# A decoder layer on one core: cache pages addressed from registers and read by SyncE, K pages one at a time, V pages in two held sets, feed-forward groups of 6, 8 and 8, last normalisation on VectorE

## The chip, the core and the metric

The kernel runs on one core of one Trainium2 chip. Its engines are TensorE (PE, matmuls, with PEld for loading the stationary operand), VectorE (DVE), ScalarE (ACT), GpSimd (POOL) and SyncE (SP, which here only issues DMAs); each runs its own list of instructions in order, and semaphores join them. The metric is the device time of one execution in microseconds, given as the median of three.

## The reference

One inference step of one layer, in float32, for 512 prompt rows and 8 sample rows (one new token each), width 1024. Every weight matrix is read once.

```python
att = _moba_prompt(aq, ak, av)                       # 8 heads of 64, blocks of 256 keys
h, (C, n, m) = _mlstm_prompt(mq, mk, mv, ig, lf)     # 4 heads of 128, log-sigmoid forget gate
mix = jnp.concatenate([att, mem], axis=-1) @ w_out
x = _layernorm(ALPHA * x + (1.0 + g1[:, None, :]) * mix, ln1_g, ln1_b)
h = x * (1.0 + sc2[:, None, :]) + sh2[:, None, :]
f = (jax.nn.silu(h @ w_gate) * (h @ w_up)) @ w_down  # D_FF = 2816
return _layernorm(ALPHA * x + (1.0 + g2[:, None, :]) * f, ln2_g, ln2_b)
```

The sample rows do the same, but their attention reads a paged cache: `cache_k[page_table]` and `cache_v[page_table]`, 4 pages of 128 keys x 8 heads x 64 for each of 8 rows. That is 32 K pages and 32 V pages of 256 KB, at addresses that are known only when the page table has been read.

## The kernel before

**The main line.** TensorE multiplies float32 numbers as three passes over a high and a low part. Each tile of weights (128 x 1024 numbers) is loaded by SyncE into one of six `raw` buffers (L185), ScalarE casts it to `whi` (L228), another engine subtracts to get `wlo` (L229), and the raw buffer is free again. L229 runs on VectorE, but for tiles 8 to 13 on GpSimd (`PT_`). The main blocks (`wstat_block` L631, `astat_block` and the products of the output and feed-forward stages, whose matmuls stand at L387) use one tile after the other: first the input projections (aq, ak, av, mq, mk, mv, mo), then the output product, then 22 feed-forward tiles with their down products in three groups of tiles (`FF_GROUPS`), then the layer normalisation of the four row tiles. Between the main tiles come side tiles of the adaLN weights (`ps_ada`).

**The lanes.** All else is written as Python generators, called lanes. A main block calls `tick()` after each of its pieces; a tick lets every lane go one `yield` further, prepares one weight tile (two ahead of the one in use) and asks for loads as raw buffers come free. So the order of instructions on each engine is fixed when the program is written, by the ticks. `yield n` waits n ticks; `slot(pool, ...)` waits until a pool has a free buffer (13 halves of 128 x 512 numbers, 22 units of twice that).

**The sample attention.** `sample_scores(b)` handles row b's K pages. It takes four halves, issues four page reads, and some ticks later gives GpSimd four multiplies by the broadcast query in a row (L1202); VectorE then sums them per head. `page` (L1183, its DMA at L1184) is an indirect DMA of GpSimd, with row numbers `idx` worked out beforehand on VectorE. `sample_attention` follows: softmax over the scores, then the products `ps_pv` of the V pages on TensorE (L1289), in eight steps (two groups of rows, four pages each). A step fetches four pages into halves that it takes when there are four free, at most two steps ahead, waits `lag_v` = 4 ticks from its fetch and gives the halves back.

**Its neighbours.** At the same time run the prompt's block attention (its transposed probabilities `ps_pt` on TensorE, copied by VectorE at L827), the mLSTM heads (`ms_unit`: rows `negM` read from DRAM by SyncE, masked by GpSimd at L1013, exponentials on ScalarE, L1027 on VectorE; `mlstm_num` for the numerators), the gates (`log_sigmoids`) and the sample rows' mLSTM states (L1331 to L1334 and L1399 on VectorE).

**The end.** `down_last` makes the last group's down product, tile after tile of rows, half after half of columns. Results are evacuated by VectorE (L1578, L1579: times the gate, plus the residual); `ln2_tile` normalises, dividing the scale and shift (`lg`, `lb`) among ScalarE, GpSimd and VectorE; `ln2_last` does the last tile, and in it one addition (L1854) for the tile before. `affine8` does the sample rows' scale and shift on GpSimd.

## Time and profile before

| what | value |
|---|---|
| median of three runs | 816.4 us (813.91 to 821.64) |
| the profiled execution, its own time | 814.67 us |
| its span, first to last instruction | 813.0 us |
| mean granted TensorE clock | 0.972 |
| busy: TensorE, VectorE, ScalarE, GpSimd | 757.7, 407.1, 277.9, 229.6 us |
| DMA | 123.10 MB, mean 151 GB/s |

In the profile, L12 is line 12 of the kernel before. A row of a timeline has the start in us, the duration in us, the engine, the line and operation with output and inputs by name, how many follow each other, and in brackets the idle time before it with what ended that. A row of groups has the count, the busy time, the mean in ns, and the idle time before. A row of a single line or tile has ns as min/median/max. A row ending in "issue" waited for nothing that the profile shows; "remote" and "another core or an unknown queue" mean that the releaser isn't among the recorded instructions. SPq is SyncE's sequencer. A row of SyncE's waits has the total in us, how often, and the longest.

### The profile page before, as it was taken

To read this page: it belongs to the slowest core of one execution; us is meant where nothing else is said; L and a number is where in the kernel's file an instruction comes from. 1 tells how busy PE (TensorE), PEld (TensorE's weight loads), DVE (VectorE), ACT (ScalarE), POOL (GpSimd) and SP (SyncE) were. 2 spreads that over 40 slices of the span, in tenths; PEclk is the share of its full clock that TensorE was granted. 3 is DMA by queue.
4 is the path that set the end of the run, shared out by engine and by line. 5 is a ranking of instruction groups with operands and counts; after the bars stand their busy time and mean duration, and the time that the engine had idled before them with its cause. 6 is when DMAs were issued, how large, how long until landed. Compare 5 with 4: busy or idle time off the path is not lost.

```text
span 813.0 us, 14321 instructions
## 1 busy us (share of the span) xinstructions
PE 757.7 (93%) x5760; PEld 621.5 (76%) x5760; DVE 407.1 (50%) x851; ACT 277.9 (34%) x555; POOL 229.6 (28%) x244
## 2 busy tenths in 40 slices
PE   5999999698989898899999999999999999999992
PEld 4788667587756575566699998789999877999772
DVE  2551667955534867367855443333333333433585
ACT  2331557434323336346462232122223212222201
POOL 2021579786140326000008700221000022100055
PEclk9999999899999899799999999999999999999997
DMA  8956775566396767646352533233323223321011
GB/s 339 358 206 212 229 251 162 159 212 204 111 290 183 210 218 216 251 148 208 106 164 78 120 116 130 80 103 92 90 80 103 78 78 104 112 96 53 1 40 67
DMA packets 101948, 123.10 MB, mean 151 GB/s; under 512 B 8362, under 2 KB 65838, under 8 KB 101882
## 3 DMA queue, kind: packets, MB, share of 16 engines
q1 hardware_dynamic: 88722, 96.27, 37.1%
q0 software_dynamic: 5184, 16.79, 6.7%
q10 hardware_dynamic: 7976, 9.13, 3.5%
q8 instruction: 45, 0.74, 0.4%
q14 instruction: 21, 0.17, 0.1%
HBM read 114.99 MB, written 7.17 MB: 150 GB/s over the span
## 4 chain that ended last, share of the span: by engine, by line
PE 77%; DVE 12%; DMA 3%; issue 2%; ACT 2%; another core or an unknown queue 1%; POOL 1%; SPq 0%; ACTq 0%; POOLq 0%; DVEq 0%
PE acc L631 35%; PE acc L387 27%; DMA vpage<-in_cache_v_dram,idx 2%; PE ps_ada L401 2%; PE ps_dn L409 1%; PE accl L387 1%; PE ps_sc L789 1%; PE ps_pt L819 1%; DVE x L1579 1%; PE ps_pv L1289 1%; PE ps_ada L455 1%; PE ps_o L842 1%; DVE wlo L229 1%; PE ps_s L401 1%
## 5 line engine op out<-in xcount | busy, mean ns | idle before, releaser
L229 DVE TENSOR_TENSOR wlo<-raw,whi 128x1024 fp32r<-128x1024 f32 x98 | 126.3, 1297 | 115.4 <-ACT whi L228 112.3
L228 ACT CAST whi<-raw 128x1024 fp32r<-128x1024 f32 x104 | 108.3, 1049 | 165.4 <-PE acc L387 80.7
L631 PE MATMUL acc<-h_hi,whi 128*128 128x256 f32 (+1 forms) x640 | 129.8, 284 | 0.0
L631 PE MATMUL acc<-h_hi,wlo 128*128 128x256 f32 (+1 forms) x640 | 128.4, 282 | 0.0
L631 PE MATMUL acc<-h_lo,whi 128*128 128x256 f32 (+1 forms) x640 | 128.2, 282 | 0.0
L631 PEld LDWEIGHTS acc<-h_hi,whi 128*128 128x128 f32 x640 | 99.2, 188 | 2.2 <-issue 2.1
L631 PEld LDWEIGHTS acc<-h_lo,whi 128*128 128x128 f32 x640 | 99.5, 188 | 0.0
L631 PEld LDWEIGHTS acc<-h_hi,wlo 128*128 128x128 f32 x640 | 98.8, 188 | 0.0
L1733 POOL COPY fsT<-vf 128x8 f32<-128x8 f32 x20 | 4.8, 241 | 192.3 <-DVE vf L1728 192.3
L387 PE MATMUL acc<-whi,f_hi 128*128 128x512 f32 x128 | 51.6, 404 | 0.0
L387 PE MATMUL acc<-whi,f_lo 128*128 128x512 f32 x128 | 50.4, 394 | 0.0
L387 PE MATMUL acc<-wlo,f_hi 128*128 128x512 f32 x128 | 50.3, 393 | 0.0
L1202 POOL TENSOR_TENSOR kpage<-kpage,qb 128x512 f32<-128x512 f32 x32 | 40.9, 1306 | 29.6 <-DMA qb<-r_scr 25.8
L1579 POOL TENSOR_TENSOR x<-x,rtmp 128x512 f32<-128x512 f32 x16 | 26.0, 1647 | 77.3 <-DVE rtmp L1578 77.0
L1727 DVE TENSOR_TENSOR vf<-acc,vf 128x256 f32<-128x256 f32 x20 | 8.5, 425 | 74.6 <-PE acc L631 74.6
L387 PE MATMUL acc<-whi,hT_hi 128*128 128x512 f32 x96 | 43.4, 452 | 0.0
L631 PE MATMUL acc<-hT_hi,whi 128*128 128x256 f32 (+1 forms) x160 | 36.8, 310 | 3.5 <-remote 1.8
L1184 POOL DMA_INDIRECT vpage<-in_cache_v_dram,idx x32 | 32.1, 1002 | 27.6 <-DVE own L1243 12.1
L1184 POOL DMA_INDIRECT kpage<-in_cache_k_dram,idx x32 | 33.1, 1035 | 21.5 <-DVE gw L898 13.0
L387 PE MATMUL acc<-wlo,hT_hi 128*128 128x512 f32 x96 | 39.0, 406 | 0.0
L387 PE MATMUL acc<-whi,hT_lo 128*128 128x512 f32 x96 | 38.8, 404 | 0.0
L393 ACT CAST f_hi<-vf 128x512 fp32r<-128x512 f32 (+1 forms) x24 | 14.0, 585 | 68.4 <-DVE vf L1728 62.4
(408 smaller groups left out, 1492.1 us busy)
## 6 DMA issues: line engine op xcount, KB each, us to landing
...
```

Of the source, the lines that this page charges most:

```text
L228: ACOPY(out=t.hi_t, in_=t.raw)
L229: (PT_ if 8 <= t.index < 14 else TT)(out=t.lo_t, in0=t.raw, in1=t.hi_t, op=ALU.subtract)
L387: mm(ps, lhsT=a, rhs=b, start=start and i == 0, stop=stop and i == n - 1)
L393: ACOPY(out=dst_hi, in_=v)
L401: mm(ps[32 * c:32 * c + 32, 0:P], lhsT=lhs[:, k0 + kk, :], rhs=raw3[:, kk, ts(c, P)], start=start and kk == 0, stop=stop and kk == nk - 1, ...
L409: mm(ps[32 * c:32 * c + 32, 0:256], lhsT=lhs[:, k0 + kk, :], rhs=raw3[:, kk, ts(n, 256)], start=start, stop=stop, tile_position=(0, 32 * c))
L455: mm(ps[32 * c:32 * c + 32, 0:w], lhsT=siluT[:, k, :], rhs=rhs, start=k == 0, stop=k == 7, tile_position=(0, 32 * c))
L631: mm(accs[d, hf][:, 0:hi - lo], lhsT=w, rhs=two(xx, k)[:, lo:hi], start=k == 0 and i == 0, stop=k == 7 and i == 2)
L1184: nc.gpsimd.indirect_dma_start(out=dst, out_offset=None, in_=src, in_offset=bass.IndirectOffsetOnAxis(ap=idx[:, 4 * b + j:4 * b + j + 1], ...
L1202: PT_(out=ks[j], in0=ks[j], in1=qb, op=ALU.mult)
L1579: (PT_ if pool_add else TT)(out=dst, in0=dst, in1=tmp, op=ALU.add)
L1727: TT(out=v[:, 0:HALF], in0=a[:, 0:HALF], in1=v[:, 0:HALF], op=ALU.mult)
```

## The change

1. **Pages.** `page` reads the page's number from the table in SBUF into a register of SyncE and issues a plain DMA at that address from SyncE. The page table is loaded as one row, and `idx` with its preparation is gone.
2. **K pages.** `sample_scores` asks for one page a tick (ticks 0 to 3 of its ten), multiplies one a tick on GpSimd (4 to 7) and sums one a tick on VectorE (6 to 9).
3. **V pages.** Two sets of four buffers (one of two units, one of four halves) are taken once. Both are filled as soon as the scores are done; set i is filled again with step i+2 right behind the products of step i. `lag_v` is 5.
4. **Subtractions.** L229 runs on VectorE for all tiles.
5. **Gates and numerators.** `log_sigmoids` uses two activations of ScalarE in place of an operation of VectorE, with one tick less; `mlstm_num` yields after both halves.
6. **Feed-forward.** The groups are 6, 8 and 8 tiles. `down_last` makes the first two row tiles together for each half of the columns, as the weights come in, and then the other two as before; three tiles ahead are prepared only from the last tile on, and splits may then use raw buffers.
7. **Last normalisation.** All four affine steps of a tile are on VectorE; the sample rows are normalised on ScalarE, with the affine on VectorE; `ln2_last` has no addition for the tile before.

On GpSimd, the part with the second half of the K pages. `kpage` is a K page's buffer, `qb` the broadcast query, `wlo` the low part of a weight tile, `gt` the gates. Before:

```order
41 L1184 DMA kpage<-in_cache_k_dram,idx 128x512 x4
42 L229 TENSOR_TENSOR wlo<-raw,whi 128x1024
43 L1202 TENSOR_TENSOR kpage<-kpage,qb 128x512 x4
44 L960 DMA out_dram<-gt_1469 4x1
45 L961 DMA m_scr<-gt_1470 4x512
46 L1184 DMA kpage<-in_cache_k_dram,idx 128x512 x4
47 L229 TENSOR_TENSOR wlo<-raw,whi 128x1024
48 L1202 TENSOR_TENSOR kpage<-kpage,qb 128x512 x4
```

The same place on GpSimd now, up to the masks of the mLSTM heads (`E`):

```order
28 L1200 TENSOR_TENSOR kpage<-kpage,qb 128x512 x20
29 L956 DMA out_dram<-gt_1604 4x1
30 L957 DMA m_scr<-gt_1605 4x512
31 L1200 TENSOR_TENSOR kpage<-kpage,qb 128x512 x12
32 L1009 TENSOR_TENSOR E<-negM,mask_t 128x128 x6
```

Page reads and subtractions are gone from GpSimd's list; the 32 multiplies follow each other with two DMAs between, each behind its own page.

On SyncE, from the gate rows of the first mLSTM head (`negM`) to those of the second. `raw` is a weight buffer, `m_...` are sample states. Before:

```order
75 L1115 DMA negM<-m_scr 128x512
76 L1391 DMA m_2545<-in_state_n_dram 8x512
77 L185 DMA raw<-in_w_in_dram 128x2x512
78 L1393 DMA m_2543<-r_scr 8x512
79 L1394 DMA m_2544<-r_scr 8x512
80 L185 DMA raw<-in_w_ada_dram 128x2x512
81 L185 DMA raw<-in_w_in_dram 128x2x512
82 L185 DMA raw<-in_w_ada_dram 128x2x512
83 L1115 DMA negM<-m_scr 128x512
```

SyncE now, the end of the same stretch; the four page reads are of the first set filled again (`pt_i` is the page table):

```order
241 L185 DMA raw<-in_w_in_dram 128x2x512
242 L1181 TENSOR_LOAD pt_i
243 L1181 ISA x2
244 L1182 ISA
245 L1182 DMA vpage<-in_cache_v_dram 128x512
246 L1181 TENSOR_LOAD pt_i
247 L1181 ISA x2
248 L1182 ISA
249 L1182 DMA vpage<-in_cache_v_dram 128x512
```

Two more pages follow in the same way, and `negM` of the second head stands behind them. A page is five instructions in SyncE's list, and weights and gate rows queue behind it.

The diff, cut:

```diff
@@ -38,7 +38,7 @@
 N_HALVES = 13
-FF_GROUPS = ((0, 8), (8, 16), (16, 22))
+FF_GROUPS = ((0, 6), (6, 14), (14, 22))

@@ -220,13 +220,15 @@
                 src_hi, src_lo = units, units
+            elif state["load"] == len(stream) and len(raws.free) >= 2:
+                src_hi, src_lo = raws, raws
             else:
...
             ACOPY(out=t.hi_t, in_=t.raw)
-            (PT_ if 8 <= t.index < 14 else TT)(out=t.lo_t, in0=t.raw, in1=t.hi_t, op=ALU.subtract)
+            TT(out=t.lo_t, in0=t.raw, in1=t.hi_t, op=ALU.subtract)
             t.hi = t.hi_t.rearrange("p (k c) -> p k c", k=t.k)
@@ -272,9 +274,6 @@
     make_identity(nc, ident)
-    iota_p = cst.tile([P, 1], F32, name="iota_p")
-    nc.gpsimd.iota(iota_p, pattern=[[0, 1]], base=0, channel_multiplier=1,
-                   allow_small_or_imprecise_dtypes=True)
     siluT = cst.tile([P, KD, 32], F32, name="siluT")
@@ -360,8 +359,7 @@
     nc.gpsimd.memset(mhalf, -0.5)
-    pt_i = cst.tile([P, 32], I32, name="pt_i")
-    idx = cst.tile([P, 32], I32, name="idx")
+    pt_i = cst.tile([1, 32], I32, name="pt_i")
     ng = cst.tile([P, 512], F32, name="ng")
@@ -369,7 +367,7 @@
     def later_loads():
-        dma(out=pt_i, in_=row_bc(page_table, 0, 32))
+        dma(out=pt_i, in_=at(page_table, 0, [[0, 1], [1, 32]]))
         dma(out=wg, in_=win[:, :, 3584:3592])
@@ -377,7 +375,6 @@
     def later_consts():
-        TS(out=idx, in0=pt_i, scalar1=128.0, scalar2=iota_p[:, 0:1], op0=ALU.mult, op1=ALU.add)
         nc.gpsimd.tensor_scalar(out=ng, in0=ng, scalar1=0.5, scalar2=None, op0=ALU.mult)
@@ -877,10 +874,9 @@
         for out, z, tmp in jobs:
-            STT(out=tmp, in0=z, scalar=-1.0, in1=z, op0=ALU.mult, op1=ALU.min)
-        yield 1
+            ACT(out=tmp, in_=z, func=AF.Abs)
         for out, z, tmp in jobs:
-            ACT(out=tmp, in_=tmp, func=AF.Exp)
+            ACT(out=tmp, in_=tmp, func=AF.Exp, scale=-1.0)
         for out, z, tmp in jobs:
@@ -1048,8 +1044,7 @@
                        start=jt == 0, stop=jt == t)
-            if half == 0:
-                yield 1
+            yield 1
         num_done[h] = True
@@ -1177,12 +1172,14 @@
     cv = cache_v.rearrange("l n p h d -> (l n p) (h d)")
+    n_phys = cache_k.shape[1]
     mixsT = cst.tile([P, KD, 32], F32, name="mixsT")
...
     def page(dst, src, b, j):
-        nc.gpsimd.indirect_dma_start(out=dst, out_offset=None, in_=src,
-                                     in_offset=bass.IndirectOffsetOnAxis(ap=idx[:, 4 * b + j:4 * b + j + 1], axis=0))
+        i = 4 * b + j
+        n = nc.sync.value_load(pt_i[0:1, i:i + 1], min_val=0, max_val=n_phys - 1)
+        dma(out=dst, in_=src[bass.ds(n * P, P), :])

@@ -1193,21 +1190,22 @@
         qb = yield from slot(halves, "qb")
-        ks = yield from slot(halves, "kpage", n=4)
         dma(out=qb, in_=row_bc(r_scr, b * 512, 512))
-        for j in range(4):
-            page(ks[j], ck, b, j)
-        yield (3, 2, 3, 2)[b // 2]
-        for j in range(4):
-            PT_(out=ks[j], in0=ks[j], in1=qb, op=ALU.mult)
-        halves.put(qb)
-        yield (2, 3, 11, 3)[b // 2]
-        for j in range(4):
-            nc.vector.tensor_reduce(out=SC[:, j, ts(b, 8)], in_=ks[j].rearrange("p (h d) -> p h d", d=64),
-                                    axis=AX, op=ALU.add)
-            halves.put(ks[j])
-            if j % 2:
-                yield 1
+        ks = []
+        for i in range(10):
+            if i < 4:
+                ks.append((yield from slot(halves, "kpage")))
+                page(ks[i], ck, b, i)
+            if 4 <= i < 8:
+                PT_(out=ks[i - 4], in0=ks[i - 4], in1=qb, op=ALU.mult)
+            if i == 7:
+                halves.put(qb)
+            if i >= 6:
+                j = i - 6
+                nc.vector.tensor_reduce(out=SC[:, j, ts(b, 8)], in_=ks[j].rearrange("p (h d) -> p h d", d=64),
+                                        axis=AX, op=ALU.add)
+                halves.put(ks[j])
+            yield 1
         sc_done[0] += 1
@@ -1220,6 +1218,18 @@
             yield 1
+        vu = yield from slot(units, "vpage", [2, 512], n=2)
+        vh = yield from slot(halves, "vpage", n=4)
+        sets = [two(vu, i) for i in range(4)], vh
+        asked = {}
+
+        def fetch(i):
+            for c in range(4):
+                page(sets[i % 2][c], cv, 4 * (i // 4) + c, i % 4)
+            asked[i] = clock[0]
+
+        fetch(0)
+        fetch(1)
         qk = yield from slot(halves, "qk8", n=2)
@@ -1273,22 +1283,19 @@
             nc.vector.memset(bank, 0.0)
-            fetched = deque()
-            j_in = 0
             for j in range(4):
-                while j_in < 4 and (not fetched or (len(fetched) < 2 and len(halves.free) >= 4)):
-                    vs = yield from slot(halves, "vpage", n=4)
-                    for c in range(4):
-                        page(vs[c], cv, 4 * g + c, j_in)
-                    fetched.append((vs, clock[0]))
-                    j_in += 1
-                while clock[0] < fetched[0][1] + lag_v:
+                i = 4 * g + j
+                while clock[0] < asked[i] + lag_v:
                     yield 1
-                vs = fetched.popleft()[0]
                 for c in range(4):
-                    mm(bank[32 * c:32 * c + 8, :], lhsT=PTs[:, j, 4 * g + c, :], rhs=vs[c],
+                    mm(bank[32 * c:32 * c + 8, :], lhsT=PTs[:, j, 4 * g + c, :], rhs=sets[i % 2][c],
                        start=j == 0, stop=False, tile_position=(0, 32 * c))
-                halves.put(vs)
+                if i < 6:
+                    fetch(i + 2)
+                elif i == 6:
+                    units.put(vu)
+                else:
+                    halves.put(vh)
                 yield 1
@@ -1666,12 +1673,12 @@

-    def affine8(xs):
+    def affine8(xs, tt, lag):
         for n in range(2):
-            PT_(out=xs[:, ts(n, 512)], in0=xs[:, ts(n, 512)], in1=big2["lg"][n][0:NB, :], op=ALU.mult)
-            yield 1
-            PT_(out=xs[:, ts(n, 512)], in0=xs[:, ts(n, 512)], in1=big2["lb"][n][0:NB, :], op=ALU.add)
-            yield 2
+            tt(out=xs[:, ts(n, 512)], in0=xs[:, ts(n, 512)], in1=big2["lg"][n][0:NB, :], op=ALU.mult)
+            yield lag
+            tt(out=xs[:, ts(n, 512)], in0=xs[:, ts(n, 512)], in1=big2["lb"][n][0:NB, :], op=ALU.add)
+            yield lag

@@ -1706,7 +1713,7 @@
                 yield 9
-                yield from affine8(xs)
+                yield from affine8(xs, PT_, 2)
                 x1_done[0] += 1
@@ -1796,10 +1803,10 @@
                 yield 2
-                TS(out=xs, in0=xs, scalar1=s[:, 12:13], scalar2=s[:, 14:15], op0=ALU.subtract, op1=ALU.mult)
-                yield 2
-                yield from affine8(xs)
-                yield 3
+                STT(out=s[:, 15:16], in0=s[:, 12:13], scalar=-1.0, in1=s[:, 14:15], op0=ALU.mult, op1=ALU.mult)
+                ACT(out=xs, in_=xs, func=AF.Identity, scale=s[:, 14:15], bias=s[:, 15:16])
+                yield 1
+                yield from affine8(xs, TT, 1)
                 dma_a(out=y_sample.rearrange("b s d -> (b s) d"), in_=xs)
@@ -1819,28 +1826,19 @@
     def ln2_tile(t):
-
         s, x = ln2_stats[t], x1[t]
...
         yield 1
-        STT(out=s[:, 27:28], in0=mean, scalar=-1.0, in1=rstd, op0=ALU.mult, op1=ALU.mult)
         g_, b_ = big2["lg"], big2["lb"]
-        xa, xb = x[:, 0:512], x[:, 512:D]
-        ACT(out=xa, in_=xa, func=AF.Identity, scale=rstd, bias=s[:, 27:28])
-        PT_(out=xa, in0=xa, in1=g_[0], op=ALU.mult)
-        PT_(out=xa, in0=xa, in1=b_[0], op=ALU.add)
-        if t == NT - 2:
-            ACT(out=xb, in_=xb, func=AF.Identity, scale=rstd, bias=s[:, 27:28])
-            PT_(out=xb, in0=xb, in1=g_[1], op=ALU.mult)
-        else:
-            STT(out=xb, in0=xb, scalar=mean, in1=g_[1], op0=ALU.subtract, op1=ALU.mult)
-            STT(out=xb, in0=xb, scalar=rstd, in1=b_[1], op0=ALU.mult, op1=ALU.add)
-            dma(out=yp[:, t, 512:D], in_=xb)
-        yield 1
-        dma_a(out=yp[:, t, 0:512], in_=xa)
+        for n in range(2):
+            xn = x[:, ts(n, 512)]
+            STT(out=xn, in0=xn, scalar=mean, in1=g_[n], op0=ALU.subtract, op1=ALU.mult)
+            STT(out=xn, in0=xn, scalar=rstd, in1=b_[n], op0=ALU.mult, op1=ALU.add)
+            (dma if n else dma_a)(out=yp[:, t, ts(n, 512)], in_=xn)
+            yield 1

@@ -1848,11 +1846,8 @@
         g_, b_ = big2["lg"], big2["lb"]
-        for lo, hi in ((0, 384), (384, 512)):
-            STT(out=x[:, lo:hi], in0=x[:, lo:hi], scalar=mean, in1=g_[0][:, lo:hi], op0=ALU.subtract, op1=ALU.mult)
-        xb = x1[t - 1][:, 512:D]
-        TT(out=xb, in0=xb, in1=b_[1], op=ALU.add)
-        dma(out=yp[:, t - 1, 512:D], in_=xb)
+        xa = x[:, 0:512]
+        STT(out=xa, in0=xa, scalar=mean, in1=g_[0], op0=ALU.subtract, op1=ALU.mult)
         STT(out=s[:, 27:28], in0=mean, scalar=-1.0, in1=rstd, op0=ALU.mult, op1=ALU.mult)
@@ -1886,8 +1881,24 @@

+
         gi = len(FF_GROUPS) - 1
-        for t in range(NT):
+        for n in range(2):
+            accs = [main_bank("accl") for _ in range(2)]
+            for q, i in enumerate(tiles[n]):
+                wt = use(i)
+                for t in range(2):
+                    prs = []
+                    for kk in range(2):
+                        k = 2 * q + kk
+                        prs += three(two(src_hi, k)[:, ts(t, P)], two(src_lo, k)[:, ts(t, P)],
+                                     wt.hi[:, kk, :], wt.lo[:, kk, :])
+                    passes(accs[t], prs, q == 0, q == len(tiles[n]) - 1)
+                    tick()
+            for t in range(2):
+                ev_down(gi, n)(t, accs[t])
+                main_put(accs[t])
+        for t in range(2, NT):
             for n in range(2):
@@ -1902,9 +1913,7 @@
                         passes(ps[:, 0:w], prs, q == 0, q == len(tiles[n]) - 1)
-                        if t == 0 and n == 0:
-                            use(tiles[1][q])
-                        elif cut == 1:
+                        if cut == 1:
                             tick()
@@ -2000,7 +2009,7 @@
     spawn(k_out(), 1)
-    spawn(sample_attention(5, 4), 1)
+    spawn(sample_attention(5, 5), 1)
     spawn(attention((3, 3, 2, 3)))
@@ -2063,9 +2072,9 @@
     for gi, (lo_f, hi_f) in enumerate(FF_GROUPS):
-        if gi == len(FF_GROUPS) - 1:
-            state["spill"] = state["lead"] = 3
         for i in range(lo_f, hi_f):
+            if i == NF - 1:
+                state["spill"] = state["lead"] = 3
             if i >= 2:
```

## The prediction

> **What bounds the kernel now.** I read the page first, then TensorE's timeline for its gaps, then for each gap the timeline of the engine that released it, and the five-microsecond windows for the clock and the DMA load.
>
> ```profile
> PE 757.7 (93%) x5760; PEld 621.5 (76%) x5760; DVE 407.1 (50%) x851; ACT 277.9 (34%) x555; POOL 229.6 (28%) x244
> PEclk9999999899999899799999999999999999999997
> ```
> TensorE is busy for 757.7 of 813.0 us, so 55.3 us of idle time and the dips of the clock row are all that a rearrangement can win. Both lie in the first half of the slices.
>
> ```profile
> 150.00:200.00 50.00, 41.37 (x362) 34.52 (x364) 33.50 (x81) 21.70 (x56) 40.52 (x33) 0.91 0.54 170
> 300.00:350.00 50.00, 40.67 (x234) 25.25 (x233) 28.35 (x81) 26.37 (x52) 14.15 (x16) 0.90 0.69 222
> 450.00:798.00 348.00, 348.00 (x2465) 311.11 (x2465) 141.37 (x180) 83.04 (x115) 55.57 (x56) 1.00 0.29 86
> ```
> Columns: length, busy time of TensorE, weight load, VectorE, ScalarE, GpSimd, granted clock, DMA share, GB/s. From 450 us TensorE has no gap at clock 1.00; nothing done to the feed-forward part can save there. The two stretches of 50 us above lose 8.6 and 9.3 us to idling, and a tenth of the clock besides. They are the attention stages, where the cache pages are read.
>
> **Part 1: the K pages and VectorE's long stall.** TensorE, then VectorE, then GpSimd, then the group of GpSimd's multiplies:
>
> ```profile
> 153.59 0.41 PE L631 MATMUL acc<-hT_lo,whi 128*128 128x256 f32 x2
> 153.84 0.40 PE L631 MATMUL acc<-hT_hi,wlo 128*128 128x256 f32 x2
> ...
> 161.08 0.69 PE L819 MATMUL ps_pt<-ident,pr 128*128 128x128 f32 x2 [6.62 <-DVE PT L827]
> ...
> 162.43 0.64 PE L631 MATMUL acc<-hT_hi,wlo 128*128 128x256 f32 x2
> 162.87 0.64 PE L631 MATMUL acc<-hT_hi,whi 128*128 128x256 f32 x2
> ```
> ```profile
> 151.44 5.89 DVE L1331 TENSOR_TENSOR ob<-ob,m0b 128x32 f32<-128x32 f32 x1
> 157.36 0.19 DVE L1332 TENSOR_TENSOR ob<-ob,gb 128x32 f32<-128x32 f32 x1
> ```
> ```profile
> 152.33 4.95 POOL L1202 TENSOR_TENSOR kpage<-kpage,qb 128x512 f32<-128x512 f32 x4
> ```
> ```profile
> L1202 POOL TENSOR_TENSOR kpage<-kpage,qb 128x512 f32<-128x512 f32 x32 | 40.9, 1306 | 29.6 <-DMA qb<-r_scr 25.8
> ```
> An operation on VectorE with two SBUF inputs took 5.89 us where its twin took 0.19, and it ended when GpSimd's four multiplies in a row ended (157.28). VectorE's copy PT comes behind it, and TensorE waits 6.62 us. Pairs of matmuls then start 0.44 us apart (162.43 to 162.87) instead of the 0.25 of 153.59 to 153.84; some six such pairs and a transposition cost 1.5 us more. The change gives GpSimd one multiply a tick (a tick is one step of the main matmul blocks) and takes the page reads and six subtractions off it. I take the whole 8.1 us away and keep back one multiply of 1.3: **−6.8**. Bounds: −8.1 if no lock is left on the path, 0 if GpSimd falls behind and its multiplies again run in a row.
>
> The six subtractions go to VectorE:
>
> ```profile
> L229 DVE TENSOR_TENSOR wlo<-raw,whi x98: 1205/1226/2316, 51.1 to 765.1; 128x1024 fp32r<-128x1024 f32 x98
> ...
> L229 POOL TENSOR_TENSOR wlo<-raw,whi x6: 2370/2376/2397, 129.4 to 187.0; 128x1024 fp32r<-128x1024 f32 x6
> ```
> 6 × 1.23 = 7.4 us on VectorE against 6 × 2.38 = 14.3 off GpSimd. VectorE was busy 33.5 of 50 us there, and the tiles are split two ahead of their use, so that lead hides them: **0**, at most +7.4.
>
> **Part 2: the V pages.** TensorE around the V reads, the chain of waits, and the windows:
>
> ```profile
> 197.40 0.39 PE L631 MATMUL acc<-hT_hi,whi 128*128 128x264 f32 x1 [1.84 <-remote]
> 197.63 0.41 PE L631 MATMUL acc<-hT_lo,whi 128*128 128x256 f32 x2
> ...
> 198.47 0.64 PE L631 MATMUL acc<-hT_lo,whi 128*128 128x256 f32 x2
> ```
> ```profile
> 239.21 1.08 PE L401 MATMUL ps_s<-raw,hsT 128*32 128x128 f32 x16 [3.48 <-DVE AT L1027]
> ```
> ```profile
> 320.36 1.03 PE L1289 MATMUL ps_pv<-vpage,vo 128*8 128x512 f32 x4
> 329.07 3.65 PE L1289 MATMUL ps_pv<-vpage,vo 128*8 128x512 f32 x4 [7.67 <-DMA vpage<-in_cache_v_dram,idx]
> ...
> 333.67 0.63 PE L387 MATMUL acc<-wlo,mixA_hi 128*128 128x512 f32 x1
> ```
> ```profile
> 231.29 7.08 another core or an unknown queue
> ...
> 310.44 18.59 DMA vpage<-in_cache_v_dram,idx
> ```
> ```profile
> 195.00:200.00 5.00, 2.99 (x28) 2.52 (x28) 0.41 (x1) 2.31 (x6) 3.12 (x3) 0.82 1.07 375
> ...
> 235.00:240.00 5.00, 1.51 (x19) 0.70 (x17) 1.33 (x2) 1.64 (x3) 1.61 (x2) 0.92 1.03 384
> ```
> One page takes 18.59 us to land and TensorE waits 7.67 us for it; the four products after it take 3.65 us instead of 1.03, and the matmuls behind are at 0.63, some 0.9 us more. That is 7.67 + 2.62 + 0.9 = 11.2 us. In the change the V reads are asked for earlier and end early: counted while the two programs are written out, the last product of a page stands at tick 83 where it stood at 103, ahead of the output stage, whose loads (prompt rows, gates, w_out) crowded in at 305 us. I take this stall away: **−11.2** (bounds −11.2 and 0, if it reappears wherever the last pages are).
>
> Against that stand the crowds. Before, eight V pages together were asked for twice, and the DMA then ran at 375 and 384 GB/s while TensorE waited 1.84 and 3.48 us, the second time behind 7.08 us of the chain in which nothing of this core is named. The change asks for eight pages within two ticks four times (ticks 59, 67–68, 72–73, 77–78): two crowds more. One costs, by the 197.40 row, 1.84 us and a slow clock after it: for an estimated 3.4 us pairs run as those after 161.08, 0.44 apart and not 0.25, which loses 1.4. Two: **+6.5** (bounds: 0, and +22.4 by the 329.07 row twice).
>
> The Trainium skill, TensorE: Matmul & The Clock Gate, Part 1, puts the fall to half clock after an idle window of about 3.4 us, and so a stop of 1.84 us need not cost any clock; by it this term would be 3.7. The trace goes against it: 0.41 becomes 0.64 one microsecond behind a stop of 1.84.
>
> **Part 3: pages on SyncE.** What a page cost GpSimd, what a plain load costs SyncE, and how SyncE waits:
>
> ```profile
> 228.01 0.95 POOL L1184 DMA_INDIRECT vpage<-in_cache_v_dram,idx  x1 [0.30 <-issue]
> ```
> ```profile
> 222.43 0.37 SPq L185 DMA_DIRECT2D raw<-in_w_in_dram  x1
> ```
> ```profile
> SPq L185 <- DVE wlo L229: 406.8, 78, 13.8
> ```
> ```profile
> L1289 PE MATMUL ps_pv<-vpage,vo x64: 592/596/1061, 225.4 to 345.5; 128*8 128x512 f32 x64
> ```
> SyncE now issues for each page a register load, three register instructions and the DMA. No row shows the first four. From below a page is 0.37; from above 1.25, what GpSimd spent with its gap. I take 0.9, between them, as nothing says which is nearer. SyncE spends most of its time waiting for a raw buffer (406.8 us), so 64 × 0.9 = 58 us fit, but not everywhere: it runs in order, and the weight loads, the gate rows negM and C states stand behind the pages, and the pages of set i+2 stand behind the products of set i on TensorE. From 225.4 to 345.5 the old program wrote 37 ticks, 3.2 us each, or about 2.5 without the waits and slow clock. Between tick 67 and 83 are 16 × 2.5 = 40 us, in which SyncE has 24 pages and some 14 other transfers at 0.4 (5.6 us). So a page may cost (40 − 5.6) / 24 = 1.4 us before TensorE waits: **0** at 0.9.
>
> The Trainium skill, DMA: Bandwidth & Descriptors, Latency and other measured facts, gives a register load of a tensor a floor of about 600 ns; with the issue a page is then an estimated 1.0 to 1.1 us, and the sum is the same. No run here shows it so far.
>
> **Part 4: the output stage and the tail.**
>
> ```profile
> 345.01 1.04 PE L1289 MATMUL ps_pv<-vpage,vo 128*8 128x512 f32 x8
> ...
> 347.96 1.04 PE L1294 MATMUL ps_pv<-vo 8*8 8x512 f32 x8
> 349.90 1.03 PE L1304 MATMUL ps_za<-sel,Z 128*128 128x4 f32 x8 [0.91 <-DVE Z L1298]
> ```
> These sample products filled TensorE while the last mLSTM head was finished. They now stand earlier, and each head's numerator yields once more, so TensorE waits there: at most the two rows that go and the tick, 1.04 + 1.03 + 2.5 = 4.6, less the 0.91 that it idled anyway; at least 0. I take **+1.5**.
>
> ```profile
> 785.26 1.71 DVE L1579 TENSOR_TENSOR x<-x,rtmp 128x512 f32<-128x512 f32 x1
> ...
> 789.65 0.75 DVE L1840 SCALAR_TENSOR_TENSOR x<-x,ls,lb 128x512 f32<-128x512 f32 x1
> 790.32 0.68 DVE L1578 TENSOR_TENSOR rtmp<-accl,G 128x512 f32<-128x512 f32 x1
> ...
> 803.07 0.68 DVE L1854 TENSOR_TENSOR x<-x,lb 128x512 f32<-128x512 f32 x1
> ```
> ```profile
> 797.95 0.28 PE L387 MATMUL accl<-wlo,f_hi 128*128 128x256 f32 x1
> 798.07 0.28 PE L387 MATMUL accl<-whi,f_lo 128*128 128x256 f32 x1
> ```
> In the last product two row tiles finish together, and VectorE has all four affine steps of a tile. With 0.68 to 0.75 an operation: sample 4 × 0.68 = 2.7; tiles 0 and 1 some 10.9 (two evacuations of three operations, 4.2 in all, small ones 0.7, eight affine steps of 0.75); tile 2 some 7.6. That is 21.2 us, while TensorE still has four blocks of 24 matmuls of 512 columns, 4 × 24 × 0.24 = 23 by the half-width ones 0.12 apart. VectorE just keeps up, with GpSimd silent (with it, 0.68 became 1.71). What surely goes is L1854 behind the last statistics: **−0.7**, up to +4 if VectorE lags. The groups of 6, 8 and 8, the streamed last product and the changed log-sigmoid move work under a full TensorE or between idle engines: 0.
>
> **Sum.** −6.8 + 0 − 11.2 + 6.5 + 0 + 1.5 − 0.7 = −10.7. The profiled execution took 814.67 us (span 813.0), 1.7 below the median of 816.4; 814.67 − 10.7 = 804.0.
>
> **Rivals.**
> *SyncE becomes the bound (slower).* If a page costs more than 1.4 us there, TensorE waits 24 times the excess in ticks 67 to 83, at the slow clock's surcharge of the 329.07 row (11.2 / 7.67 = 1.46). At 2.2 us: 24 × 0.8 × 1.46 = 28, in place of the crowds' 6.5: 804 + 21.5 = 825.5. It turns the sign from about 1.9 us a page (24 × 0.5 × 1.46 = 17.5, 11 over the 6.5), and from 2.2 by over 1%. For it: one queue for weights and pages; against: 0.37 for a load and the long waits for buffers. With it goes the same wait caused by pages that hold weights back behind a buffer. Chance 0.18.
> *The stops follow the pages (no change).* If a crowd costs as the 329.07 row, not as the 197.40 row, three crowds in a row give twice 11.2 in place of 6.5: 804 + 16 = 820; with one such, 809. For it: all engines stop together at 231 to 238 and 320 to 329; against: the first crowd cost only 1.84. The Trainium skill, Runtime: NRT & Kernel Launch, Instruction fetch mechanics, says that each engine's sequencer fetches its instructions through a DMA queue; by that rule a stop follows a DMA crowd wherever the pages are issued, and the price would be the one just given. Chance 0.2.
> *The lock stays (the change does not do what it says).* GpSimd's multiplies pile up behind late pages and run in a row: 804 + 6.8 = 811. Chance 0.08.
> *All stops go.* No crowd costs anything and the 239.21 wait goes too: 804 − 6.5 − 3.5 − 1.4 of clock = 792.6. Chance 0.09.
>
> **How the numbers follow.** The forecast has 0.45. A change under about 1% cannot be told from none; around 816.4 that is 808 to 824.5. Faster: the forecast nearly whole, all of the last rival and a little of the others, 0.60; the middle takes most of the second and third, 0.22; slower 0.18. The range from 790 to 828 leaves out little below and pages of more than 2.3 us above.
>
> **What would show it.** Part 1: no operation of VectorE over 2 us between 125 and 190 us, and no TensorE wait for PT above 1.5. Part 2: the last sample product before 300 us, no wait named vpage; waits of about 2 us with DMA above 370 GB/s. Part 3: SyncE's rows per page at 0.6 to 1.2. Tail: under the 15 us that now lie between the last matmul and the end of the span. A wait named vpage or raw at the third or fourth crowd would make the prediction wrong, as would a page above 1.4 us.

## The result and the profile after

The changed kernel takes 796.93 us (median of four, 793.95 to 797.56) where the kernel before takes 817.47 in the same session: a ratio of 0.974 with a 95% interval of 0.9686 to 0.9793. The forecast was 804. Repeated on a second chip the gain is smaller: 795.78 against 803.96, 0.9884 (0.9855 to 0.9913). The changed kernel takes the same time on both; it is the kernel before that differs by 13 us. Both pairs are needed to see what the change is worth. Why the kernel before differs is not shown.

The page after: busy times, clock, DMA share in 40 slices.

```profile
PE 752.8 (95%) x5766; PEld 621.1 (78%) x5766; DVE 409.3 (51%) x860; ACT 276.8 (35%) x555; POOL 136.5 (17%) x162
...
PEclk9999999999979999989999999999999999999998
DMA  9965874664677956926443334323222323223011
```

GpSimd lost 93 us of work, 229.6 to 136.5. TensorE's busy time fell by 4.9 us, with a mean granted clock of 0.984 in place of 0.972, and its idle time from 55.3 to 795.4 − 752.8 = 42.6. To see where, I cut each span at TensorE's first matmul of the next stage (read from its timeline). The rows of this table are durations in us; "chip 2" is the later pair of profiles.

| stage | before | after | difference | before, chip 2 | after, chip 2 | difference |
|---|---|---|---|---|---|---|
| start, aq, ak, av | 121.31 | 120.83 | −0.5 | 119.21 | 123.32 | +4.1 |
| mq, mk (K pages) | 93.30 | 84.87 | −8.4 | 88.69 | 83.98 | −4.7 |
| mv, mo (V pages) | 90.64 | 97.38 | +6.7 | 85.23 | 97.94 | +12.7 |
| output product, attention half | 34.54 | 20.64 | −13.9 | 34.41 | 20.65 | −13.8 |
| output product, mLSTM half | 23.82 | 27.99 | +4.2 | 24.32 | 27.79 | +3.5 |
| second half of the columns | 37.70 | 36.57 | −1.1 | 37.69 | 36.55 | −1.1 |
| feed-forward | 397.04 | 398.45 | +1.4 | 397.05 | 398.46 | +1.4 |
| behind the last matmul | 14.65 | 8.67 | −6.0 | 14.60 | 8.61 | −6.0 |
| span | 813.0 | 795.4 | −17.6 | 801.2 | 797.3 | −3.9 |

From the output product on the differences repeat to within 0.1 us, or 0.7 in one, gains and losses alike; the first three do not. From mv to the end of the columns' second half the change gains 4.1 us on the first chip (186.7 to 182.6) and loses 1.3 on the second (181.7 to 182.9): there the mv and mo stage loses as much as the output product saves. The two profiles of chip 2 are 3.9 us apart where the medians are 8.2 apart, so single profiles there carry some 4 us of chance; in them the end of the kernel (6.0) is more than the whole gain.

TensorE's long waits after the change, in its timeline:

```profile
149.81 0.51 PE L628 MATMUL acc<-hT_hi,whi 128*128 128x256 f32 x2 [2.02 <-DVE mixA_lo L850]
...
217.72 0.19 PE L1258 MATMUL ps_so<-ident,own 8*64 8x8 f32 x1 [4.47 <-DVE own L1255]
...
227.93 0.43 PE L1276 MATMUL ps_sp<-ident,Pm 64*128 64x64 f32 x4 [2.13 <-DVE Pm L1272]
230.13 1.33 PE L1291 MATMUL ps_pv<-vpage,vo 128*8 128x512 f32 x8 [1.72 <-DVE ps_pv L1285]
...
260.08 0.50 PE L384 MATMUL acc<-whi,hT_hi 128*128 128x512 f32 x1 [2.13 <-DVE mv L991]
...
338.61 1.65 PE L1162 MATMUL ps_C<-mk,gv 128*128 128x128 f32 x6 [4.61 <-ACT gv L1155]
```

The 6.62 us for PT and the 7.67 us for a V page are gone. New are a stop of 4.47 us for `own` (the sample rows' own scores), a pair behind it, 2.13 us for `mv`, and 4.61 us for `gv` in the output stage. SyncE's timeline shows where a part of the first comes from, and its rows at the lines of the page give what a page costs there:

```profile
202.79 9.49 SPq L1182 DMA_DIRECT2D vpage<-in_cache_v_dram  x8
212.38 0.34 SPq L1239 DMA_DIRECT2D qk<-r_scr  x1
212.76 0.30 SPq L1240 DMA_DIRECT2D qk<-s_scr  x1
213.10 0.30 SPq L1241 DMA_DIRECT2D vo<-s_scr  x1
213.45 0.35 SPq L1110 DMA_DIRECT2D negM<-m_scr  x1
...
246.20 3.91 SPq L1182 DMA_DIRECT2D vpage<-in_cache_v_dram  x4
```
```profile
L1181 SPq TENSOR_LOAD <-pt_i x64: 263/269/1067, 84.0 to 271.1; - x64
L1181 SPq FUSED_REGOPS  x64: 152/152/181, 85.0 to 271.4; - x64
```

Four pages take 3.91 us from the first DMA to the end of the last, so a page is (3.91 − 0.34) / 3 = 1.19 us: 0.27 for the register load, 0.15 for register arithmetic, 0.34 for the DMA, the rest small instructions and gaps. In the first eight it is (9.49 − 0.34) / 7 = 1.31. The loads `qk`, from which `own` is made, stand behind these eight, and TensorE stands still from 213.3 to 217.7. VectorE waits for `qk` during only 2.10 us of that:

```profile
215.69 0.68 DVE L1249 TENSOR_TENSOR qk<-qk,qk 8x512 f32<-8x512 f32 x1 [2.10 <-DMA qk<-s_scr]
```

VectorE in the K stage has its longest operation here, which answers to the 5.89 us of before; below it are two rows of GpSimd's multiplies:

```profile
159.67 3.65 DVE L231 TENSOR_TENSOR wlo<-raw,whi 128x1024 fp32r<-128x1024 f32 x1
```
```profile
120.70 7.50 POOL L1200 TENSOR_TENSOR kpage<-kpage,qb 128x512 f32<-128x512 f32 x6 [4.34 <-DMA kpage<-in_cache_k_dram]
...
156.01 6.22 POOL L1200 TENSOR_TENSOR kpage<-kpage,qb 128x512 f32<-128x512 f32 x5
```

The change meant one multiply a tick, but GpSimd waits for late pages and then runs six and five in a row: the multiplies aren't spread. VectorE's operation is still held up (1.23 alone) inside the row of five, which ends at 162.23. But it is a weight split, two tiles ahead of its use, and no long wait of TensorE follows.

Behind the last matmul the unexpected row is at the very end, at the line of the program's closing instructions. Before, then after (ns, min/median/max):

```profile
L2140 POOLq DRAIN  x3: 40/160/6308, 805.5 to 812.7; - x3
```
```profile
L2149 POOLq DRAIN  x3: 34/98/1071, 791.5 to 795.0; - x3
```

GpSimd's queue takes 6.31 us to drain before the kernel can end, and 1.07 after.

### The profile page after: what moved, and what is told of

Its sections match the earlier page's. It is cut to its first block, busy times and chain, and to the rows that moved or that the text cites. A ratio compares the mean times of both kernels' runs of the same rounds, so it can differ in the third digit from the quotient of the medians.

```text
span 795.4 us, 14629 instructions
## 1 busy us (share of the span) xinstructions
PE 752.8 (95%) x5766; PEld 621.1 (78%) x5766; DVE 409.3 (51%) x860; ACT 276.8 (35%) x555; POOL 136.5 (17%) x162
## 4 chain that ended last, share of the span: by engine, by line
PE 79%; DVE 11%; DMA 3%; issue 2%; ACT 2%; POOL 1%; SPq 0%; ACTq 0%; POOLq 0%; DVEq 0%
PE acc L628 35%; PE acc L384 28%; PE ps_ada L398 2%; PE ps_dn L406 1%; PE accl L384 1%; PE ps_num L1045 1%; DVE wlo L231 1%; PE ps_sc L786 1%; PE ps_pv L1291 1%; PE ps_o L839 1%; PE ps_pt L816 1%; PE ps_ms L1022 1%; PE ps_ada L452 1%; DVE st L792 1%; DVE rtmp L1585 1%
## 5 line engine op out<-in xcount | busy, mean ns | idle before, releaser
L231 DVE TENSOR_TENSOR wlo<-raw,whi 128x1024 fp32r<-128x1024 f32 x104 | 138.7, 1340 | 124.2 <-ACT whi L230 124.1
L384 PE MATMUL acc<-whi,f_hi 128*128 128x512 f32 x112 | 45.3, 405 | 0.0
L384 PE MATMUL acc<-whi,f_lo 128*128 128x512 f32 x112 | 44.1, 394 | 0.0
L384 PE MATMUL acc<-wlo,f_hi 128*128 128x512 f32 x112 | 44.1, 394 | 0.0
L628 PEld LDWEIGHTS acc<-hT_hi,whi 128*128 128x128 f32 x160 | 24.7, 188 | 13.7 <-issue 9.0
L628 PE MATMUL acc<-hT_lo,whi 128*128 128x256 f32 (+1 forms) x160 | 32.2, 283 | 0.0
```

What stands on the lines that cost most here:

```text
L231: TT(out=t.lo_t, in0=t.raw, in1=t.hi_t, op=ALU.subtract)
L384: mm(ps, lhsT=a, rhs=b, start=start and i == 0, stop=stop and i == n - 1)
L628: mm(accs[d, hf][:, 0:hi - lo], lhsT=w, rhs=two(xx, k)[:, lo:hi], start=k == 0 and i == 0, stop=k == 7 and i == 2)
```

## The experiments

I held two theories. A: the K stage gains because the multiplies no longer run four in a row, the output product because the V pages are asked for earlier, and who issues the pages counts only for the drain. B: the page reads of GpSimd were themselves the harm. The next four runs were made in a session where the kernel before takes 805.77 us and the changed kernel was not run; in the three sessions where it was, it took 795.78 to 797.27.

**Pages back to GpSimd, all else as changed.**

```diff
     def page(dst, src, b, j):
-        n = nc.sync.value_load(pt_i[0:1, i:i + 1], min_val=0, max_val=n_phys - 1)
-        dma(out=dst, in_=src[bass.ds(n * P, P), :])
+        nc.gpsimd.indirect_dma_start(out=dst, out_offset=None, in_=src, in_offset=...idx...)
```

> The changed kernel with its pages read by GpSimd's indirect DMAs again; the spread of the K pages, the two held V sets and all else stay. Theory A (what counts is how the multiplies are spread and how early the V pages are asked for; who issues the pages matters only at the end of the kernel, where GpSimd's last drain took 6.3 us before and 1.1 after): the stage up to 206 us and the one from 303 us stay short, the stop of 4.47 us at 217.72 goes, since weights and gate rows no longer stand behind pages in SyncE's queue, and the drain is long again: 796.9 + 5 - 4 = 797 to 800. Theory B (the page reads of GpSimd were themselves the harm, by blocking VectorE or by landing late): most of the 8.4 and 13.9 us of the two stages come back: 808 to 818.

800.25 us, 0.9945 of the kernel before (0.9924 to 0.9965) in a session where that took 805.77. Its last matmul ends at 785.92 and the span at 797.8. TensorE's wait for `own`, then GpSimd's drain:

```profile
216.41 0.17 PE L1262 MATMUL ps_so<-ident,own 8*64 8x8 f32 x1 [1.98 <-DVE own L1259]
```
```profile
L2153 POOLq DRAIN  x3: 40/102/6308, 790.7 to 797.6; - x3
```

The output product is as short as in the changed kernel (302.43 to 323.08) and no wait for a page is there, so early asking does not need SyncE. The stop for `own` is 2.5 us shorter than with SyncE (it was expected to go), and the drain is back to 6.31. Behind the last matmul it takes 11.9 us in place of 8.7.

**Pages to SyncE, all else as before.**

```diff
-        nc.gpsimd.indirect_dma_start(...)
+        n = nc.sync.value_load(pt_i[0:1, i:i + 1], min_val=0, max_val=n_phys - 1)
+        dma(out=dst, in_=src[bass.ds(n * P, P), :])
```

> The kernel before with nothing changed but the page reads, now SyncE's with page numbers in registers; K pages in fours, V pages as before. Theory A: the multiplies still stand four in a row, so a wait of TensorE of about 6 us between 150 and 165 us stays, and the V pages are as late as before, so a wait for a V page beyond 300 us stays too; only the drain at the end gets short: 817.5 - 5 = 812. Theory B: both stalls go, 817.5 - 5 - 8 - 11 = 793 to 800.

805.61 us against 805.77: no difference (0.9974 to 1.0015). TensorE's timeline:

```profile
151.65 2.07 PE L784 MATMUL ps_sc<-kT,qT 64*128 64x512 f32 x2 [1.66 <-ACT pr L794]
...
325.21 2.55 PE L1287 MATMUL ps_pv<-vpage,vo 128*8 128x512 f32 x5 [11.01 <-DMA vpage<-in_cache_v_dram]
```

The wait for a V page stays and is longer (11.01 us): here theory A holds. But the long wait in the K stage is gone although the multiplies still stand in fours: here A fails. What the shorter end saves (10.9 us behind the last matmul, against 14.6; only the pages' issuer differs, so this 3.7 is the drain's) is lost in the mv and mo stage, 93.0 us (206.37 to 299.40) against 85.2 in the profile of before on that kind of chip.

**The old V scheme, with SyncE.** The changed kernel with `fetched` and four halves at a time, lag 4, as before.

```diff
-        fetch(0)
-        fetch(1)
...
+                while j_in < 4 and (not fetched or (len(fetched) < 2 and len(halves.free) >= 4)):
+                    vs = yield from slot(halves, "vpage", n=4)
```

> The changed kernel with the V pages fetched as before (four halves at a time when they are free, lag 4), but by SyncE. Theory A (the late asking made the 7.67 us wait): the last sample product is again beyond 300 us, and a wait of 5 to 11 us for a V page comes back there: 802 to 808. Theory B (the software DMA landed late): no wait named vpage over 2 us, and without crowds a little better than the changed kernel: 793 to 798.

800.62 us (0.9931 of before, 0.9909 to 0.9954). TensorE:

```profile
317.99 2.55 PE L1287 MATMUL ps_pv<-vpage,vo 128*8 128x512 f32 x5 [9.37 <-DMA vpage<-in_cache_v_dram]
```

The time is between the two theories' (802 to 808, 793 to 798). With this and the one before, the wait beyond 300 us follows the late asking, whoever issues the pages. Its mv and mo stage is short, though, 85.7 us (208.24 to 293.97) like before's, and not 97: the held sets pay back there most of what they win later. No wait for `gv` over 1 us is left in its output stage.

**The last normalisation as before.** `ln2_tile`, `ln2_last` and the sample rows' affine are the old ones.

```diff
-            STT(out=xn, in0=xn, scalar=rstd, in1=b_[n], op0=ALU.mult, op1=ALU.add)
+        PT_(out=xa, in0=xa, in1=g_[0], op=ALU.mult)
+        PT_(out=xa, in0=xa, in1=b_[0], op=ALU.add)
```

> The changed kernel with the last normalisation and the sample rows' affine shared out among ScalarE, GpSimd and VectorE as before. Theory A (of the 6.0 us that the tail behind the last matmul lost, 3.6 are GpSimd's drain and the rest is VectorE no longer held up by GpSimd's reads): 796.9 + 2.4 = 799, the drain stays at 1.1 us, and additions of 1.1 to 1.7 us stand again in VectorE's last rows. Rival (all of it is the drain): 797.

797.90 us (0.990 of before, 0.9852 to 0.9948). From the last matmul to the end it takes 797.0 − 787.61 = 9.4 us, 0.7 more than the changed kernel's 8.67, where 2.4 were expected. VectorE's evacuation is held up again, but only now and then:

```profile
785.39 1.54 DVE L1936 TENSOR_TENSOR x<-x,rtmp 128x256 f32<-128x256 f32 x1
786.96 0.43 DVE L1937 BATCH_NORM_STATS2 ls<-x 128x6 f32<-128x256 f32 x1
787.65 0.42 DVE L1935 TENSOR_TENSOR rtmp<-accl,G 128x256 f32<-128x256 f32 x1 [0.26 <-PE accl L384]
```

By the last piece it waits for TensorE again, and the last DMA is issued 5.86 us behind the last matmul, where the changed kernel does so after 5.66. So the move of the affine is worth 0.2 us. The other 0.5 is the time from that DMA to the end, which in runs with the new normalisation and the short drain varies too, from 2.9 to 3.7 us.

**The kernel before, on the second chip**, unchanged:

> The kernel before, looked at again on another chip, where its median is 806 and not 817 us. If the stall at 151 to 161 us and the 7.67 us wait for a V page are properties of the program, both are there again and the difference of 11 us lies elsewhere; if the stall depends on how two queues happen to meet, one of them is smaller or gone. Expected: the V page's wait of 7 to 11 us stays, the first stall is under 3 us.

TensorE, then VectorE:

```profile
157.98 0.69 PE L819 MATMUL ps_pt<-ident,pr 128*128 128x128 f32 x2 [6.63 <-DVE PT L827]
...
317.59 3.42 PE L1289 MATMUL ps_pv<-vpage,vo 128*8 128x512 f32 x4 [8.69 <-DMA vpage<-in_cache_v_dram,idx]
```
```profile
148.33 5.89 DVE L1331 TENSOR_TENSOR ob<-ob,m0b 128x32 f32<-128x32 f32 x1
```

Both stalls are there, to a hundredth of a microsecond in the first, so they belong to the program; I had expected the first to shrink. What is missing on this chip is the other kind: of the stops without a releaser, 197.40 is gone and the wait for AT is 1.30 in place of 3.48. The table has the difference, 2.1, 4.6 and 5.4 us in the first three stages, and little behind them.

**The changed kernel, on the second chip**, unchanged:

> The changed kernel beside the others on this chip, so that their ratios can be compared. If the gain of 20 us holds on every chip: 0.974 of the kernel before, 785. If the kernel before merely met its stalls more often on the first chip: 0.985 to 0.995.

795.78 us, 0.9884: near the second of the two ratios expected.

**A dearer page.** The changed kernel with each register load four times.

```diff
         n = nc.sync.value_load(pt_i[0:1, i:i + 1], min_val=0, max_val=n_phys - 1)
+        for _ in range(3):
+            nc.sync.value_load(pt_i[0:1, i:i + 1], min_val=0, max_val=n_phys - 1)
         dma(out=dst, in_=src[bass.ds(n * P, P), :])
```

> The changed kernel with each page's register load done four times, so that a page costs SyncE about 0.45 us more for each extra load: from 1.2 to some 2.5 us. By the rival 'SyncE becomes the bound' with its limit of 1.4 us a page: 24 x 1.1 x 1.46 = 39 us more than the changed kernel, mostly as waits for V pages. If the true limit is higher (V pages asked earlier than they are needed): 5 to 15 us more, and mainly at the first crowd, where small loads stand behind eight pages: 8 x 1.3 = 10.

848.04 us, 52.3 more than the changed kernel beside it. SyncE, then TensorE:

```profile
215.16 20.53 SPq L1184 DMA_DIRECT2D vpage<-in_cache_v_dram  x8
235.79 0.33 SPq L1241 DMA_DIRECT2D qk<-r_scr  x1
```
```profile
240.38 0.19 PE L1260 MATMUL ps_so<-ident,own 8*64 8x8 f32 x1 [16.45 <-DVE own L1257]
...
276.05 1.03 PE L1293 MATMUL ps_pv<-vpage,vo 128*8 128x512 f32 x2 [1.91 <-DMA vpage<-in_cache_v_dram]
```

A page is now (20.53 − 0.33) / 7 = 2.89 us, more than I had meant. The rival's formula with that price gives 24 × (2.89 − 1.4) × 1.46 = 52 us, the amount measured, but that is partly luck. The formula counts waits for V pages alone, and eight of them come to 12.1 us; 12.5 of the loss is the stop for `own` (16.45 against 3.97), and the K stage is 9 us longer (216.38 − 123.31 against 83.98), with slow clock behind some of it. At this price SyncE's queue bounds these stages; where between 1.3 and 2.9 us a page it starts to do so, no run shows.

**Small loads first.** The first eight V pages behind the sample rows' three small loads, the second four of them behind the gate rows.

```diff
-        fetch(0)
-        fetch(1)
         qk = yield from slot(halves, "qk8", n=2)
...
         dma(out=c4(v8), in_=s_tok(2))
+        fetch(0)
...
-        yield 4
+        yield 2
+        fetch(1)
+        yield 2
```

> The changed kernel with the first eight V pages asked for behind the three small loads of the sample rows (four pages at once behind them, four two ticks later, behind the gate rows). If the stop of 4.47 us at 217.72 is the small loads' place in SyncE's queue behind eight pages of 1.2 us: it goes, and with the slow clock behind it 5 to 7 us less than the changed kernel. If it is the DMA crowd itself: no difference.

793.14 us, 0.986 of before (0.9823 to 0.9896), 2.6 less than the changed kernel beside it; the intervals of the two ratios overlap. TensorE:

```profile
214.81 0.17 PE L1259 MATMUL ps_so<-ident,own 8*64 8x8 f32 x1 [2.39 <-DVE own L1256]
```

The stop is shorter by 1.6 to 2.1 us, not gone: with the loads issued at once it is about what it was with the pages on GpSimd. So the queue order is half of the stop, as the 2.10 us for `qk` said. The rest is in ScalarE's and VectorE's lists:

```profile
210.42 1.05 ACT L230 CAST whi<-raw 128x1024 fp32r<-128x1024 f32 x1 [1.85 <-DMA r_scr<-row_sb]
```
```profile
211.50 1.23 DVE L231 TENSOR_TENSOR wlo<-raw,whi 128x1024 fp32r<-128x1024 f32 x1 [5.26 <-ACT whi L230]
```

ScalarE casts a weight tile only behind writes of the sample rows to DRAM that it issues itself (`r_scr`). VectorE stands 5.26 us for that cast, and the operations that make `own` are next in its list. The changed kernel has the same pair of rows at 211.28 and 212.36.

**The changed kernel as a measure for the last three**, on a chip where the kernel before takes 817.33:

> The changed kernel once more, as the measure for the other three on this chip: 794 to 798, 0.97 to 0.99 of the kernel before, depending on how the kernel before does on it.

797.27 us, 0.9765 (0.9715 to 0.9815).

**K pages in fours, pages with SyncE.**

```diff
-        for i in range(10):
-            if i < 4:
-                ks.append((yield from slot(halves, "kpage")))
-                page(ks[i], ck, b, i)
...
+        ks = yield from slot(halves, "kpage", n=4)
+        for j in range(4):
+            page(ks[j], ck, b, j)
+        yield (3, 2, 3, 2)[b // 2]
+        for j in range(4):
+            PT_(out=ks[j], in0=ks[j], in1=qb, op=ALU.mult)
```

> The changed kernel with K pages, multiplies and sums in fours as before; pages stay with SyncE. Theory 'multiplies in a row' (the price in the prediction): an operation of VectorE of over 4 us comes back between 125 and 190 us, and a wait of TensorE of 4 to 7 us for PT with it: 6 to 8 us more than the changed kernel, 802 to 804. Theory 'who stands next' (the experiment that only moved the pages kept the fours and had no operation over 3.1 us there): the row of four costs only when an urgent operation meets it, and the time stays within 3 us of the changed kernel.

798.03 us, 0.9781 (0.9731 to 0.9831): 0.8 from the changed kernel, inside the noise. The K stage is 85.66 us, against 83.74 in the run beside it. GpSimd, then TensorE:

```profile
133.80 6.48 POOL L1199 TENSOR_TENSOR kpage<-kpage,qb 128x512 f32<-128x512 f32 x4 [8.86 <-DMA kpage<-in_cache_k_dram]
144.77 7.21 POOL L1199 TENSOR_TENSOR kpage<-kpage,qb 128x512 f32<-128x512 f32 x4 [4.49 <-DMA kpage<-in_cache_k_dram]
...
155.63 4.99 POOL L1199 TENSOR_TENSOR kpage<-kpage,qb 128x512 f32<-128x512 f32 x4
```
```profile
148.16 0.51 PE L628 MATMUL acc<-hT_hi,whi 128*128 128x256 f32 x2 [2.29 <-DVE mixA_lo L850]
```

The rows of four are back, two of them now stretched themselves, to 6.48 and 7.21 us from 4.99, and no wait for PT follows. Theory A's first half falls; but this run is a weak test of spread multiplies, since the changed kernel runs them in rows too. The operation that took 5.89 us before stands in the row of 7.21 us here:

```profile
149.52 1.27 DVE L1337 TENSOR_TENSOR ob<-ob,m0b 128x32 f32<-128x32 f32 x1
```

It meets a row of four again and loses some 1.1 us, not 5.7. So a meeting of the two is not enough for the stall. The runs with pages off GpSimd, with the new order of multiplies, and with both are all free of it; what decides whether VectorE's operation gets in between two multiplies or stands until the row ends is not shown.

**V pages on GpSimd, K pages with SyncE.**

```diff
+        if src is cv:
+            nc.gpsimd.indirect_dma_start(...)
+        else:
             n = nc.sync.value_load(...)
```

> The changed kernel with the V pages alone read by GpSimd's indirect DMAs (32 in place of 64 before) and the K pages by SyncE. For the drain: if GpSimd's last drain grows with the number of its indirect DMAs, about half of the way from 1.07 to 6.31, that is 3.7 us; if any such DMA costs all, 6.3. For SyncE: the stop of 4 us at the small loads behind eight pages gets 2 us shorter, as with all pages on GpSimd. Together the time of the changed kernel, within 2 us, for 3.7, or 2 to 3 more for 6.3.

805.19 us, 0.9864 (0.9803 to 0.9924), 7.9 more than the changed kernel, where at most 3 were expected. The drain:

```profile
L2158 POOLq DRAIN  x3: 40/107/3697, 798.6 to 802.8; - x3
```

3.70 us for 32 indirect DMAs lies on the line through 1.07 for none of the pages and 6.31 for 64: 0.082 us each. The stop for `own` is 1.78 us, shorter as expected. I had counted the rest of the time wrong: the K stage is 89.99 us against 83.74. In it stands the first crowd of V pages. Windows of five microseconds (columns as in the prediction), then TensorE:

```profile
185.00:190.00 5.00, 5.00 (x56) 4.80 (x54) 3.62 (x10) 3.67 (x8) 3.78 (x5) 1.00 1.03 399
190.00:195.00 5.00, 3.02 (x23) 1.79 (x12) 2.16 (x3) 0.49 (x3) 2.43 (x3) 0.91 0.75 208
195.00:200.00 5.00, 5.00 (x35) 4.36 (x34) 0.00 (x0) 2.72 (x6) 0.00 (x0) 0.50 0.77 218
```
```profile
190.91 0.28 PE L633 MATMUL acc<-hT_hi,whi 128*128 128x264 f32 x1 [0.35 <-issue]
191.62 0.49 PE L633 MATMUL acc<-hT_lo,whi 128*128 128x256 f32 x2 [0.44 <-issue]
192.34 0.28 PE L633 MATMUL acc<-hT_hi,wlo 128*128 128x256 f32 x1 [0.22 <-issue]
193.05 0.38 PE L633 MATMUL acc<-hT_hi,wlo 128*128 128x264 f32 x1 [0.43 <-issue]
```

Behind a crowd at 399 GB/s matmuls come one at a time, with gaps in which TensorE waits for nothing that the profile names, and the clock halves. That looks like the stop of the prediction's 197.40 row. The rate alone doesn't bring it. First a window of the run with all pages on GpSimd, on a chip where the kernel before takes 806, then one of the changed kernel with its pages on SyncE, on the first chip:

```profile
190.00:195.00 5.00, 5.00 (x64) 4.30 (x63) 2.58 (x4) 3.50 (x9) 3.79 (x4) 1.00 1.04 386
```
```profile
265.00:270.00 5.00, 5.00 (x40) 3.48 (x42) 1.76 (x3) 0.41 (x2) 0.00 (x0) 1.00 1.05 398
```

TensorE is busy throughout both, at clock 1.00. The nameless stops show only with V pages on GpSimd and in sessions where the kernel before takes 817 us. The Trainium skill, Runtime: NRT & Kernel Launch, Instruction fetch mechanics, has the sequencers fetch their instructions through DMA queues; the gaps fit that, but no run here shows the fetch itself.

**A faster version.** Small loads first, as above, and the numerators' second yield undone.

```diff
-            yield 1
+            if half == 0:
+                yield 1
         num_done[h] = True
```

> A version for speed: the small loads of the sample rows before the V pages, as in the earlier run that gained 2.6 us, and the numerators' second yield undone, which brings the last mLSTM head one tick earlier. If the wait of 4.6 us for gv in the output stage follows the last head's chain: 1.5 to 3 us of it go, and with the first part the time is 4 to 6 us under the changed kernel, about 791. If the chain is not what is late: 793 to 794.

794.28 us, 0.9737 (0.9698 to 0.9776), 3.0 under the changed kernel by the medians; the intervals overlap. It is the fastest of its session. TensorE in the output stage:

```profile
332.29 1.36 PE L1094 MATMUL ps_hm<-ident,hm 128*128 128x128 f32 x4 [2.17 <-ACT hm L1076]
```

The 4.61 us for `gv` have become 2.17 for the last head's `hm`, and the mLSTM half takes 27.2 us (319.58 to 346.77) and not 28.0. So by the trace the wait follows the last head's chain, but one tick gives back 0.8 us of the stage, less than expected; by the time alone, 794.28, the run would count for the other case (793 to 794).

## Why the prediction was right or wrong

**The direction, the range and the largest gain were right.** Measured 796.93 lies between 790 and 828, and 7 below the forecast of 804.

**Part 1, the K pages: −6.8 forecast; −8.4 and −4.7 measured in the stage; the reason was wrong.** The stall went as a whole (5.89 us and the wait for PT). But the step that gave it to one multiply a tick failed: the multiplies run in rows of up to six in the changed kernel, and with the fours restored the time changed by 0.8. The condition of the rival "the lock stays" came true, and its cost didn't. Why the stall went is open.

That −8.4 is near −6.8 is partly luck: the 1.84 us stop at 197.40, which the prediction counted with the crowds, lies in this stage too. The second chip's kernel before has no such stop, its stage is 4.6 us shorter, and the gain there is 4.7. A wait of 2.0 us for `mixA_lo` at 150 is new on both chips. The 4.1 us of the stage ahead are chance: the small-loads-first run, the same program up to there, took 120.77 us for it on that chip. The subtractions on VectorE, forecast at nothing, were not taken back in any run; no long wait follows them in the trace, but each of the four operations over 2 us there is one of VectorE's splits, and the prediction had named one such operation as a sign against Part 1.

**Part 2, the V pages: −11.2 forecast; −13.9 and −13.8 measured in the output product's first half; right.** Two experiments in which the pages are late have the wait again (11.01 and 9.37 us), with SyncE as the issuer; the one with early pages on GpSimd has none. Some of the 13.9 is products that moved into the stage before.

**The crowds: +6.5 forecast, +6.7 measured on the first chip; right in size by luck, wrong in mechanism.** No stop without a releaser is left in the changed kernel, although SyncE's crowds move up to 398 GB/s in five microseconds, where GpSimd's moved 375 and 384. What TensorE waits for is the small loads behind eight pages, and a chain of ScalarE and VectorE beside that. On the second chip the stage costs 12.7: there the kernel before has hardly any crowd stops to set against it.

**Part 3, SyncE: 0 at 0.9 us a page; the page is 1.19 to 1.31 us, of six instructions and not five.** It stayed under the limit of 1.4, so the rival did not come to decide, but it was nearer than I gave it: at 2.89 us a page the kernel loses 52 us. The Trainium skill, DMA: Bandwidth & Descriptors, Latency and other measured facts, puts a register load at no less than about 600 ns. Here the load itself took 0.27 us, less than that; with its arithmetic and gaps each further load of the dearer page cost some 0.55, (2.89 − 1.19) / 3 = 0.57 or (2.89 − 1.31) / 3 = 0.53. The rival had the place only half right; the first thing to be late was not a V page but what stands in line behind one.

**Part 4, the output stage: +1.5 forecast, +4.2 and +3.5 measured.** The size was at the upper bound of 4.6: the wait for `gv` is 4.61. The mechanism is right: with the old V scheme that wait is 0.97 us, and without the second yield it gives way to 2.17 for `hm`, though the stage gets only 0.8 us shorter.

**The tail: −0.7 forecast, −6.0 measured on both chips. This is the term that failed.** GpSimd's drain falls from 6.31 to 1.07 us. Not all of it was exposed: from the last DMA's issue to the end it is 813.0 − 806.35 = 6.65 before and 795.4 − 792.39 = 3.01 after, 3.6 less. The two runs that change only the issuer of the pages give 3.7 (from the kernel before) and 3.3 (from the changed one). The other 2.3 lie between the last matmul and that DMA: VectorE's last evacuation began 1.97 us behind the last matmul before, and begins 0.03 behind it now. It is 1.96 in the run that changes only the issuer, and 0.04 with the old normalisation put back, so by exclusion this part belongs to the new groups and the new order of the last product; no run undid these alone. The affine with L1854, the only part of the tail that was priced, at 0.7, is worth 0.2. The drain stood in the trace of before, at the closing line, in a row that I did not ask for: I followed TensorE and VectorE to their last instruction and not GpSimd's queue.

**The feed-forward: 0 forecast, +1.4 measured**, the same on both chips; no experiment took it apart. It comes with the new groups and the new order of the last product in every run, so some 1.4 of the tail's gain may only have moved across the cut.

Of the rivals, "the lock stays" fell in its cost, and "the stops follow the pages" fell too: no stop like the 329.07 row came, at up to 398 GB/s. "All stops go" gave 792.6, nearer to the result than the forecast is, but the stops did not go: they were 4.47, 2.13, 1.72 and 4.61 us, and the drain made up for them. The Trainium skill, TensorE: Matmul & The Clock Gate, Part 1, was weighed over a stop of 1.84 us; in the changed kernel the stop of 4.47 us at 217.72 is longer than its idle window of about 3.4 us and has matmuls of 0.63 us behind it in place of 0.39, so that row does not decide between the two.
